# Unit tiles staggered by 64 bytes in on-chip memory, in a two-layer hybrid encoder

## The chip, the cores and the metric

The kernel runs on one core of one Trainium2 chip. The metric is the device time of one execution in microseconds (us), as the median of several runs. A profiled execution has a time of its own and a span, from its first to its last recorded instruction.

## The reference

The input x has 512 positions of 1024 float32 values. After a LayerNorm two layers follow, each with a mixing and a channel part:

```
h = layer_norm(x)
for l in 2 layers:
    proj = h @ w_in[l]                 # split into the inputs of four groups of 256 columns
    a = GLU -> depthwise conv of width 31 -> LayerNorm -> silu
    b = attention, 4 query and 2 key heads of 64, RMS norm, 2-D rotary
    c = gated unit: u * (sgu_w @ LN(v) + bias), in chunks of 128 positions
    d = attention with low-rank q and k/v, 4 heads of 96
    h = LN(alpha * h + concat(a, b, c, d) @ w_out[l])
    up = depthwise conv of width 3 (h @ ffn_w_up[l])       # 2 x 2816 columns
    h = LN(alpha * h + (silu(up[:, :2816]) * up[:, 2816:]) @ ffn_w_down[l])
```

## The kernel before, in words

**Products.** Every large product is made three times from numbers split in two: `split` (ACT copies a float32 tile into a rounded tile `hi`; DVE, or POOL for a few, subtracts to get the rest, `lo`), and `mm3` (three matmuls on TensorE: hi x hi, hi x lo, lo x hi, into one PSUM bank). The normalised stream stands transposed in `hh` and `hl` (128 partitions, 8 blocks of 512). In the feed-forward's first product (`ffn`, `col_mm`) a weight slice of 128 columns is the stationary operand (`wh`, `wl`) and a block of `hh` or `hl` the moving one, 512 columns long. In the second (`residual`, weights "W") the activations `fh` and `fl` are stationary and the weights move; part of these weights is kept in `hh` and `hl`, which are free by then (`load`). In attention, `att_pv` takes a 128-column slice of the value tile `bv` as the stationary operand; `b_attention` begins it at element 64*pr of the 192 elements that a key head has, so at bytes 0, 768, 256 and 1024 of the tile.

**Memory.** `Kern.__init__` opens pools in this order: const (with `h0` to `h3`), raws (3 slots of 4096 bytes per partition, where weights land from HBM), small, units, the two PSUM pools, and splits (`hh`, `hl`). The pool of units has 69 slots (`SLOTS["u"]`), nearly all other tiles live in it: split weights, activations, probabilities, row vectors. A tile never exceeds 2048 bytes per partition. In the compiled program of before, slot i begins at byte 53888 + 2048*i of each partition, so every unit begins 640 bytes past a multiple of 2048; `h0` to `h3` and the blocks of `hh` and `hl` begin at 640 too, the three raw slots at 1696.

**Order.** `Sched` records all operations, and `place` lays them out on five engines with costs, ranks and a window; it chooses the slot of each tile from a list of free slots that starts in the order of their numbers. `issue` then takes each tile from its pool under the tag of its slot (`u0` to `u68`, one buffer each) and issues the operations in the planned order, every one from the same line, L460. Planning takes no account of addresses.

Of the kernel before, what the change touches and what calls it, by code (L numbers as in the profile page):

```python
# [9 lines left out]
F32 = mybir.dt.float32  # L10
# [6 lines left out]
P = 128  # L17
# [39 lines left out]
SLOTS = {"u": 69, "raw": 3, "acc": 4, "wk": 4, "s": 48}  # L57
# [59 lines left out]
class View:  # L117


    def __init__(self, t, p0, p1, arr, chain):  # L120
        self.t, self.p0, self.p1, self.arr, self.chain = t, p0, p1, arr, chain
# [350 lines left out]
class Kern:  # L472
    def __init__(self, ctx, tc, x, wst, sguw, pp, rows, tabs, incol, out):
        nc = tc.nc
        self.x, self.wst, self.sguw, self.rows, self.out = x, wst, sguw, rows, out
        cp = ctx.enter_context(tc.tile_pool(name="const", bufs=1))
        PS = bass.MemoryType.PSUM
        pools = {"raw": ctx.enter_context(tc.tile_pool(name="raws", bufs=1)),
                 "s": ctx.enter_context(tc.tile_pool(name="small", bufs=1)),
                 "u": ctx.enter_context(tc.tile_pool(name="units", bufs=1)),  # L480
                 "acc": ctx.enter_context(tc.tile_pool(name="accs", bufs=1, space=PS)),
                 "wk": ctx.enter_context(tc.tile_pool(name="wks", bufs=1, space=PS))}

        sp = ctx.enter_context(tc.tile_pool(name="splits", bufs=1))
        self.s = Sched(tc, {k: (p, 0) for k, p in pools.items()})
        ident = cp.tile([P, P], F32, name="ident")
        make_identity(nc, ident)

        def fixed(shape, dt, name):
            return VTile(None, shape, dt, name, cp.tile(shape, dt, name=name))  # L490
        self.ident = VTile(None, [P, P], F32, "ident", ident)
        self.h = [fixed([P, DM], F32, f"h{t}") for t in range(NT)]
        self.hh, self.hl = [VTile(None, [P, KD, S], FR, n, sp.tile([P, KD, S], FR, name=n)) for n in ("hh", "hl")]
        self.pp, self.tabs = fixed([P, L * NPP], F32, "pp"), fixed([P, NT, 192], F32, "tabs")
        self.incol, self.incol_in = fixed([P, 2 * KD], F32, "incol"), incol
        self.pp_in, self.tabs_in = pp, tabs
        self.loaded = {}
# [846 lines left out]
```

## Time and profile before

| | |
|---|---|
| median of three runs | 1199.14 us (1197.52 to 1200.43) |
| profiled execution, its own time | 1199.15 us |
| its span | 1197.3 us |
| instructions | 15703, of which 5778 matmuls and 5778 weight loads |
| granted TensorE clock, mean | 0.991 |

PE is TensorE's matmuls, PEld its weight loads, DVE VectorE, ACT ScalarE, POOL GpSimd. The span counts from the first instruction recorded; the time of the execution is a little longer. In a timeline a matmul's duration covers its whole way through the array, so that the durations of neighbours overlap; what a matmul takes from the engine is the distance between starts.

### The profile page before, as it was taken

What the parts mean: (1) busy time and instruction counts of PE and PEld (TensorE: products, weight loads), DVE (VectorE), ACT (ScalarE), POOL (GpSimd) and SP (SyncE); (2) the same over time, 40 slices, a digit from 0 to 9 for tenths busy, and PEclk for the clock granted to TensorE, in tenths of its full rate; (3) what the DMA queues carried; (4) which work ended last, traced back from release to release, by engine and by line L of the source; (5) the groups of instructions that cost most, each with busy time, mean ns of one, the idle gap of its engine ahead of it and who ended that gap; (6) DMA issues with size and microseconds to landing.
All of it is one profiled execution on the core that took longest, in us unless ns stands there. A gap on an engine that the chain in (4) does not pass through costs nothing.

```text
span 1197.3 us, 15703 instructions
## 1 busy us (share of the span) xinstructions
PE 1147.8 (96%) x5778; PEld 962.6 (80%) x5778; DVE 830.4 (69%) x1546; ACT 558.1 (47%) x1193; POOL 216.0 (18%) x242
## 2 busy tenths in 40 slices
PE   5999998999999999999999999899999999999997
PEld 4787776898888888888898877779888888888886
DVE  8799899787666555525487999979766666661426
ACT  4657686335444443413224679752544444441221
POOL 5245666200000000000001467530000000000001
PEclk8999999999999999999999999999999999999999
DMA  8410211223422222333421201121333323331311
GB/s 301 134 54 1 88 54 54 89 71 123 141 88 97 81 71 75 122 103 108 139 80 62 71 1 53 37 88 54 124 105 98 96 90 105 100 97 50 106 53 71
DMA packets 32044, 105.74 MB, mean 88 GB/s; under 512 B 3680, under 2 KB 4064, under 8 KB 31968
## 3 DMA queue, kind: packets, MB, share of 16 engines
q1 hardware_dynamic: 31968, 104.74, 27.0%
q8 instruction: 45, 0.74, 0.3%
q14 instruction: 31, 0.25, 0.1%
HBM read 102.63 MB, written 2.10 MB: 87 GB/s over the span
## 4 chain that ended last, share of the span: by engine, by line
PE 77%; DVE 16%; ACT 4%; issue 2%; POOL 1%; DMA 0%; SPq 0%; DVEq 0%; ACTq 0%; POOLq 0%
PE acc L460 50%; PE wk L460 27%; DVE aconv L460 5%; DVE ptl L460 2%; DVE max L460 2%; DVE nu L460 1%; DVE wl L460 1%; DVE ny L460 1%; ACT by L460 1%; DVE h L460 1%; ACT prob L460 1%; POOL bw L460 1%; ACT pth L460 0%; DVE c L460 0%; DVE bst L460 0%
## 5 line engine op out<-in xcount | busy, mean ns | idle before, releaser
L460 DVE TENSOR_TENSOR wl<-raw,wh 128x512 fp32r<-128x512 f32 (+1 forms) x264 | 174.0, 690 | 64.9 <-ACT wh L460 50.2
L460 ACT ACTIVATE wh<-raw 128x512 fp32r<-128x512 f32 (+2 forms) x310 | 176.4, 615 | 43.6 <-DMA raw<-in_wst_dram 21.7
L460 PE MATMUL acc<-hl,wh 128*128 128x512 f32 (+1 forms) x544 | 191.6, 352 | 1.7 <-DVE hl L460 1.6
L460 PE MATMUL acc<-hh,wh 128*128 128x512 f32 (+1 forms) x544 | 191.8, 353 | 0.2 <-ACT hh L460 0.2
L460 PE MATMUL acc<-hh,wl 128*128 128x512 f32 (+1 forms) x544 | 191.3, 352 | 0.0
L460 POOL TENSOR_TENSOR wl<-raw,wh 128x512 fp32r<-128x512 f32 (+1 forms) x46 | 62.9, 1384 | 472.9 <-ACT wh L460 459.9
L460 PE MATMUL wk<-hh,wh 128*128 128x512 f32 x320 | 124.5, 389 | 0.0
L460 PE MATMUL wk<-hl,wh 128*128 128x512 f32 x320 | 124.5, 389 | 0.0
L460 PE MATMUL wk<-hh,wl 128*128 128x512 f32 x320 | 124.5, 389 | 0.0
L460 PEld LDWEIGHTS acc<-hl,wh 128*128 128x128 f32 x544 | 102.8, 189 | 16.4 <-DVE hl L460 2.6
L460 PEld LDWEIGHTS acc<-hh,wh 128*128 128x128 f32 x544 | 102.8, 189 | 14.3 <-ACT hh L460 0.5
L460 PEld LDWEIGHTS acc<-hh,wl 128*128 128x128 f32 x544 | 102.8, 189 | 13.7
L460 DVE SCALAR_TENSOR_TENSOR y<-acc,pp,y 128x511 f32<-128x511 f32 x96 | 71.9, 749 | 55.3 <-ACT y L460 54.0
L460 DVE TENSOR_TENSOR hl<-raw,hh 128x512 fp32r<-128x512 f32 x56 | 38.1, 691 | 93.2 <-ACT hh L460 93.2
L460 DVE SCALAR_TENSOR_TENSOR aconv<-aglu,pp,aconv 128x502 f32<-128x502 f32 (+14 forms) x120 | 94.6, 811 | 0.3
L460 DVE SCALAR_TENSOR_TENSOR y<-wk,pp,y 128x511 f32<-128x511 f32 x80 | 59.9, 749 | 46.2 <-ACT y L460 45.1
L460 PE MATMUL acc<-hl,fh 128*128 128x512 f32 x224 | 85.8, 383 | 0.0
L460 PE MATMUL acc<-hh,fh 128*128 128x512 f32 x224 | 85.7, 383 | 0.0
L460 PE MATMUL acc<-hh,fl 128*128 128x512 f32 x224 | 85.7, 382 | 0.0
L460 ACT ACTIVATE hh<-raw 128x512 fp32r<-128x512 f32 x56 | 34.8, 630 | 107.2 <-PE acc L460 66.1
L460 POOL TENSOR_TENSOR prob<-prob,rec 128x512 f32<-128x512 f32 x64 | 71.5, 1130 | 54.2 <-DVE rec L460 44.8
L460 POOL TENSOR_TENSOR h<-h,row 128x512 f32<-128x512 f32 x6 | 9.3, 1576 | 389.4 <-DVE h L460 389.4
(194 smaller groups left out, 2436.4 us busy)
## 6 DMA issues: line engine op xcount, KB each, us to landing
raw<-in_wst_dram SPq DMA_DIRECT2D x172, 512.0 KB, 3.5
row<-in_rows_dram SPq DMA_DIRECT2D x16, 256.0 KB, 6.4
raw<-in_wst_dram SPq DMA_DIRECT2D x8, 352.0 KB, 3.2
out_dram<-h SPq DMA_DIRECT2D x8, 256.0 KB, 2.0
h<-in_x_dram SPq DMA_DIRECT2D x3, 512.0 KB, 5.3
raw<-in_wst_dram SPq DMA_DIRECT2D x2, 384.0 KB, 3.9
h<-in_x_dram SPq DMA_DIRECT2D x2, 256.0 KB, 3.0
sgurow<-in_rows_dram SPq DMA_DIRECT2D x2, 256.0 KB, 5.8
```

The costliest lines, as they stand in the source:

```text
L460: f(*[a.real() if isinstance(a, View) else a for a in args], **{k: v.real() if isinstance(v, View) else v for k, v in kw.items()})
```

## The change

A loop behind the pools takes, ahead of all other tiles, one tile of 2048 bytes for each slot of the pool of units, under the slot's tag, and after slots 2, 5, 8, ... 59 a further tile of 64 bytes under a tag of its own. Neither is written or read. Slot i thus lies 64 bytes further for every such tile ahead of it: slots 0 to 2 as before, 3 to 5 by 64 bytes, and so on to slots 60 to 68 by 1280. The pool of splits, which follows, moves by 1280 bytes.

```diff
@@ -480,6 +480,11 @@
                  "u": ctx.enter_context(tc.tile_pool(name="units", bufs=1)),
                  "acc": ctx.enter_context(tc.tile_pool(name="accs", bufs=1, space=PS)),
                  "wk": ctx.enter_context(tc.tile_pool(name="wks", bufs=1, space=PS))}
+
+        for i in range(SLOTS["u"]):
+            pools["u"].tile([P, 512], F32, tag=f"u{i}", name=f"home{i}", bufs=1)
+            if i % 3 == 2 and i < 60:
+                pools["u"].tile([P, 16], F32, tag=f"gap{i}", name=f"gap{i}", bufs=1)
 
         sp = ctx.enter_context(tc.tile_pool(name="splits", bufs=1))
         self.s = Sched(tc, {k: (p, 0) for k, p in pools.items()})
```

## Rows read from the trace of the kernel before

**Rows 1.** The page: busy us and instructions by engine; the chain that ended last.

```profile
PE 1147.8 (96%) x5778; PEld 962.6 (80%) x5778; DVE 830.4 (69%) x1546; ACT 558.1 (47%) x1193; POOL 216.0 (18%) x242
...
PE 77%; DVE 16%; ACT 4%; issue 2%; POOL 1%; DMA 0%; SPq 0%; DVEq 0%; ACTq 0%; POOLq 0%
```

**Rows 2.** The table of stretches: a mixing stage and the two feed-forward stages.

```profile
core 0: us, PE busy (x) PEld busy (x) DVE busy (x) ACT busy (x) POOL busy (x), PEclk, DMA share, GB/s
100.00:200.00 100.00, 90.66 (x518) 74.61 (x518) 94.52 (x196) 73.53 (x171) 61.03 (x64) 0.97 0.17 53
250.00:600.00 350.00, 349.41 (x1626) 292.53 (x1625) 198.20 (x306) 135.44 (x222) 0.00 (x0) 1.00 0.32 104
850.00:1150.00 300.00, 300.00 (x1347) 249.29 (x1347) 168.39 (x249) 120.74 (x197) 0.00 (x0) 1.00 0.31 98
```

**Rows 3.** Timeline of PE, 400 to 410 us: the first and last of 44 starts.

```profile
start us, us, engine line op out<-in xcount [idle before <-releaser]
400.03 0.39 PE L460 MATMUL acc<-hh,wh 128*128 128x512 f32 x1
400.25 0.39 PE L460 MATMUL acc<-hl,wh 128*128 128x512 f32 x1
400.48 0.39 PE L460 MATMUL acc<-hh,wl 128*128 128x512 f32 x1
...
409.77 0.39 PE L460 MATMUL wk<-hl,wh 128*128 128x512 f32 x1
```

**Rows 4.** The table of stretches again: two short ones, at either level of the clock.

```profile
14.00:18.60 4.60, 4.60 (x13) 3.62 (x12) 4.04 (x8) 1.63 (x3) 4.60 (x5) 0.50 0.99 371
400.00:410.00 10.00, 10.00 (x45) 8.26 (x44) 5.28 (x8) 4.87 (x8) 0.00 (x0) 1.00 0.20 73
```

**Rows 5.** Timeline of PE, 14.2 to 19.9 us; six starts left out.

```profile
15.02 0.63 PE L460 MATMUL wk<-wh,hl 128*128 128x512 f32 x1
15.45 0.63 PE L460 MATMUL wk<-wh,hh 128*128 128x512 f32 x1
...
18.01 0.63 PE L460 MATMUL wk<-wh,hh 128*128 128x512 f32 x1
18.44 0.63 PE L460 MATMUL wk<-wl,hh 128*128 128x512 f32 x1
...
19.25 0.39 PE L460 MATMUL wk<-wh,hh 128*128 128x512 f32 x1
19.48 0.40 PE L460 MATMUL wk<-wl,hh 128*128 128x512 f32 x1
19.72 0.39 PE L460 MATMUL wk<-wh,hl 128*128 128x512 f32 x1
```

**Rows 6.** Instructions on tiles fh, fl, hh and hl: count, duration ns min/median/max.

```profile
L460 ACT ACTIVATE fh<-y x44: 615/633/634, 273.0 to 1073.5; 128x512 fp32r<-128x512 f32 x44
L460 DVE TENSOR_TENSOR fl<-y,fh x44: 678/692/694, 273.7 to 1074.2; 128x512 fp32r<-128x512 f32 x44
...
L460 ACT ACTIVATE hh<-raw x56: 615/632/634, 499.6 to 1144.2; 128x512 fp32r<-128x512 f32 x56
L460 DVE TENSOR_TENSOR hl<-raw,hh x56: 674/693/694, 500.3 to 1144.8; 128x512 fp32r<-128x512 f32 x56
```

**Rows 7.** Timeline of PE, attention times values, 702.3 to 704.1 us; four starts left out.

```profile
702.87 0.28 PE L460 MATMUL wk<-pth,bv 128*128 128x256 f32 x1
702.99 0.28 PE L460 MATMUL wk<-ptl,bv 128*128 128x256 f32 x1
703.11 0.28 PE L460 MATMUL wk<-pth,bv 128*128 128x256 f32 x1
703.23 0.28 PE L460 MATMUL wk<-ptl,bv 128*128 128x256 f32 x1
...
703.83 0.28 PE L460 MATMUL wk<-pth,bv 128*128 128x256 f32 x1
703.95 0.28 PE L460 MATMUL wk<-ptl,bv 128*128 128x256 f32 x1
```

## The prediction

> **What bounds the kernel now.** I read the page's busy shares and its chain first, then a table of stretches, then the TensorE timeline inside one stretch, because a change of addresses alone can act only through the length of single instructions. PE is busy for 96% of the span and the chain that ended last is 77% PE; DVE holds 16% of it [rows 1]. The table shows two stretches, 250 to 600 us and 850 to 1150 us, which are the two feed-forward stages: PE is busy for 649.4 of 650 us there, while DVE works 56% of the time, ACT 39% and POOL not at all [rows 2]. Nothing but the matmul rate sets the time of these 650 us. In the attention and convolution stages the same table has DVE at 94.5% and PE at 90.7% (100 to 200 us), so a gain of PE alone would be only partly paid there [rows 2].
>
> What one matmul costs is its pitch, the time from one start to the next; the duration in the timeline is longer because matmuls overlap. From 400.03 to 409.77 us there are 44 starts of 512-column matmuls, so 43 steps in 9.74 us: 226.5 ns each [rows 3]. In this stretch the granted clock was 1.00, the 2.4 GHz level [rows 4]; 512 columns at one per cycle are 213.3 ns. So each matmul carries about 13.3 ns more than its columns (226.67 ns is 544 cycles, and the starts are that regular). From 14.0 to 18.6 us the granted clock was 0.50, the 1.2 GHz level [rows 4], and eight steps from 15.02 to 18.44 us take 427.5 ns each, against 426.7 ns for 512 columns at that rate: within the rounding of the starts there is no surplus [rows 5]. The 13.3 ns therefore exists only when the moving operand streams at the full rate. That is the one place in this trace where operand addresses could be at work: a weight load (PEld, 80% busy beside PE's 96% [rows 1]) runs next to the matmuls, and both read the same partitions.
>
> **The change, part by part.** *The home tiles.* They fix slot i of the pool as the i-th 2048 bytes. The slots were already 2048 bytes apart and were first taken in the order of their numbers (the planner's free list starts sorted), so slot i keeps its place apart from the gaps. No instruction writes or reads a home or gap tile, so the real tile that follows one in a slot finds nothing to wait for; the planner never sees them, so order, slots, DMAs and semaphores stay. Cost 0, with nothing moved past any queue. If a tile did wait, it would be once per slot, at its first use, and there is no earlier work in the slot to wait on.
>
> *The gaps.* There are 20 of 64 bytes. Slot i shifts by 64 times the number of gaps ahead of it, and the last pool (hh, hl) by 1280. Before, every unit, hh, hl and every row block of h started 640 bytes past a multiple of 2048. Afterwards a unit's phase is 640 + 64g, with g from 0 to 20, and hh and hl have 1920.
>
> *DVE, ACT and POOL.* Their operands change phase against each other. The trace has both arrangements already. In fl<-y,fh all three operands have one phase; in hl<-raw,hh the source lies 1056 bytes off. DVE's medians are 692 and 693 ns; ACT's, for fh<-y and hh<-raw, 633 and 632 ns [rows 6]. A relative shift costs or gives under 1 ns in these pairs, so I enter 0. The bounds are plus and minus 1 ns on 1546 DVE instructions [rows 1], that is 1.5 us, were all of them on the path.
>
> *DMA.* Starts stay multiples of 64 bytes, the weight stream goes to the unshifted raw pool, and the DMA engines are 20% busy in the stretch of [rows 4] at 400 us. Cost 0; if a transfer took longer, a share of this size hides it.
>
> *TensorE against the other engines.* In the 10 us of [rows 3] DVE was busy for 5.28 and ACT for 4.87 us [rows 4], on units of the very same phase as the operands that PE reads, and the pitch did not move. I see no collision to remove here: 0.
>
> *TensorE against itself.* This is the open term. Afterwards the moving operand and the stationary one mostly have different phases. The nearest row is the attention's product with the values. There the stationary slice of the second head begins 768 bytes further into its tile than that of the first, with the moving tiles in the same phase. The first head's last step (702.87 to 702.99 us) and the second's seven from 703.11 to 703.95 us are all 120 ns [rows 7]. That is 106.7 ns for 256 columns at full rate and the same 13.3 ns; so a shift of 768 bytes leaves the surplus exactly, and so does halving the columns. Shifts of 64, 128 and 192 bytes have no row. The bounds: from minus 13.3 ns per matmul (the surplus goes) to plus 13.3 ns (it doubles). On the 5778 matmuls [rows 1] that is 77 us either way, an upper bound that also counts the transposes. I take the nearest row: 0.
>
> A page of the Trainium skill would set the floor elsewhere. TensorE: Matmul & The Clock Gate, section "Wait — 56ns, not 53.3ns?", gives N ÷ 2.4 GHz plus about 2.5 ns for back-to-back matmuls, 215.7 ns at 512 columns. The trace here disagrees, with 226.5 ns; its estimate for the half rate (426.7 ns) agrees. If the difference of 10.8 ns were all due to the phases and went in all 2973 matmuls of the two stretches, the kernel would be 32 us faster; that is rival A with this page's floor.
>
> **Sum:** 0 + 0 + 0 + 0 against the profiled execution's 1199.15 us (span 1197.3 and 1.85 us around it), which equals the median of the three runs, 1199.14, to 0.01 us. I forecast 1199.1 us.
>
> **The rivals.** *A, the surplus goes (faster).* Moving operand and weights collide in some unit of memory because their phases are equal, and different phases part them. For it: the surplus shows at the full rate alone, as a clash of two readers would. Against it: it is the same to the nanosecond for 256 and 512 columns and for the 768-byte shift, which looks like a fixed cost of changing weights. Price: since 768 bytes change nothing, a power of two at which phases repeat is at most 256; of the 69 slots 24 then still agree with hh and hl (g = 0, 4, 8, 12, 16 with three slots each, and the nine from slot 60 on), 45 differ, 65%. Of 2973 matmuls in the two PE-bound stretches [rows 2] that is 2973 x 0.65 x 13.3 ns = 25.7 us; over all 5778, 50 us. So 1149 to 1173 us, about 1165 with the other stages paying half. Were only one phase in three relieved, 9 us in the two stretches: 1190 us.
>
> *B, the shifted phases clash more (slower).* The weights of the next matmul are fetched while the moving operand streams; with equal phases the two may now keep out of each other's way for most of the time. Pitches above 227 ns do occur: 230 and 240 ns just after the clock rose, from 19.25 to 19.72 us [rows 5]. If half the surplus again, 6.7 ns, fell on the 65%, that is 2973 x 0.65 x 6.7 ns = 12.9 us in the two stretches: 1212 us. It decides once the pitch rises by 0.8 ns on average (2.4 us over 2973). Against it, again, the 768-byte row.
>
> *C, the change does not do what it says.* Should the allocator round or reorder slots so that the phases stay equal, the time is 1199 us as well; I give it 0.03, which lies inside the forecast's chance.
>
> **How the numbers follow.** A measurement of this kernel can tell about 0.2% (2.4 us) from no change; the three runs span 0.24%. No effect, C included, gets 0.72: the rows of DVE, ACT and the 768-byte shift all say that phases do not matter, but none of them has a 64-byte step. A gets 0.17, its full size 0.11 and its small one 0.06; B gets 0.11, of which about half would end under 1208 us. The likeliest case alone spans 1196.5 to 1201.8 us. To leave out no more than 2 in 10, the range takes in A's small form and B's smaller half: 1188 to 1208 us, which leaves out 0.11 and about 0.06.
>
> **What would show it.** Right: in 400 to 410 us of the new trace the step is again 226.5 ns with 44 or 45 starts; the loads, the medians of fl, hl, fh and the two fully busy stretches keep their lengths to 0.2%. A would show as steps between 213 and 220 ns for some weights and 226.5 for others, and B as steps of 230 ns or more, with PE still busy throughout. A new wait ahead of the first tile of a slot, or DVE medians off by more than 1 ns, would prove the other zeros wrong.

## The result, and the profile after

The changed kernel takes 1212.4 us (median of four runs, 1211.37 to 1214.8) against 1199.77 us before (median of four runs by then): a ratio of 1.0111 with a 95% interval of 1.0091 to 1.0132. (The ratio is estimated from the single runs; the two medians alone give 1.0105.) It is slower by 12.6 us, and the time lies above the range's upper end of 1208 us. I had forecast no change; what came is rival B, at its price of 1212 us.

The page of the changed kernel, busy us by engine and the shares of the chain that ended last:

```profile
PE 1161.5 (96%) x5778; PEld 961.3 (79%) x5778; DVE 830.1 (69%) x1546; ACT 558.3 (46%) x1193; POOL 215.8 (18%) x242
...
PE 80%; DVE 14%; ACT 3%; issue 2%; POOL 1%; DMA 0%; SPq 0%; DVEq 0%; ACTq 0%; POOLq 0%
```

Against [rows 1], PE has changed: 13.7 us more, with the same 5778 matmuls. The weight loads have 1.3 us less; DVE, ACT and POOL agree to 0.3 us, and PE's share of the chain has gone from 77 to 80%. The span grew by 13.3 us, from 1197.3 to 1210.6. The table of stretches shows it as a lower rate:

```profile
core 0: us, PE busy (x) PEld busy (x) DVE busy (x) ACT busy (x) POOL busy (x), PEclk, DMA share, GB/s
...
250.00:600.00 350.00, 349.41 (x1595) 287.64 (x1594) 193.00 (x291) 135.32 (x222) 0.00 (x0) 1.00 0.32 104
850.00:1150.00 300.00, 300.00 (x1336) 245.31 (x1335) 167.84 (x247) 119.33 (x194) 0.00 (x0) 1.00 0.29 93
```

PE waits no more than before [rows 2] and the granted clock is 1.00 in both, but fewer matmuls fit. The timeline of PE from 400 to 410 us, first and last of the starts and a few between:

```profile
400.19 0.40 PE L460 MATMUL acc<-hl,wh 128*128 128x512 f32 x1
400.42 0.40 PE L460 MATMUL acc<-hh,wl 128*128 128x512 f32 x1
400.67 0.40 PE L460 MATMUL acc<-hh,wh 128*128 128x512 f32 x1
...
402.75 0.39 PE L460 MATMUL acc<-hh,wh 128*128 128x512 f32 x1
402.97 0.39 PE L460 MATMUL acc<-hl,wh 128*128 128x512 f32 x1
...
409.91 0.40 PE L460 MATMUL wk<-hl,wh 128*128 128x512 f32 x1
```

The 42 steps from 400.19 to 409.91 us average 231.4 ns where [rows 3] have 226.5, and they are no longer equal: 250 ns in one place and 220 in another, in the rows shown. I took the same instructions out of both traces, by their place in PE's order: the 2743 matmuls of 512 columns that lie in the two stretches of the kernel before have a mean pitch of 226.8 ns there and of 231.2 ns now. That is 4.5 ns each and 12.3 us together, of the 13.3 us by which the span grew. Sorted by the distance between the weights that are being loaded and the operand that is moving (addresses from the compiled program, modulo 256), the means away from the stages' borders are 230.1 ns at 0, 232.8 at 64, 232.4 at 128 and 230.5 at 192; before, all were at 0 with 226.7. Where the border is drawn moves these means by about 0.2 ns. The matmuls at distance 0 are of two kinds: in 260 to 590 and 860 to 1140 us, the 415 that come straight after another distance average 232.6 ns, and the 223 with seven or more at distance 0 in front of them 226.7.

The zeros entered for the other engines stand. Instructions on hh, hl, fh and fl, duration min/median/max:

```profile
L460 ACT ACTIVATE fh<-y x44: 614/632/634, 271.9 to 1084.8; 128x512 fp32r<-128x512 f32 x44
L460 DVE TENSOR_TENSOR fl<-y,fh x44: 681/692/695, 272.5 to 1085.4; 128x512 fp32r<-128x512 f32 x44
...
L460 ACT ACTIVATE hh<-raw x56: 612/632/635, 502.6 to 1156.9; 128x512 fp32r<-128x512 f32 x56
L460 DVE TENSOR_TENSOR hl<-raw,hh x56: 674/692/694, 503.3 to 1157.6; 128x512 fp32r<-128x512 f32 x56
```

The medians of [rows 6] are met to 1 ns.

### The profile page after: what moved, and what is told of

Same layout as the page of the kernel before. It is cut to its first block, busy times and chain, and to the rows that moved or that the text cites. A ratio compares the mean times of both kernels' runs of the same rounds, so it can differ in the third digit from the quotient of the medians.

```text
span 1210.6 us, 15703 instructions
## 1 busy us (share of the span) xinstructions
PE 1161.5 (96%) x5778; PEld 961.3 (79%) x5778; DVE 830.1 (69%) x1546; ACT 558.3 (46%) x1193; POOL 215.8 (18%) x242
## 4 chain that ended last, share of the span: by engine, by line
PE 80%; DVE 14%; ACT 3%; issue 2%; POOL 1%; DMA 0%; SPq 0%; DVEq 0%; ACTq 0%; POOLq 0%
PE acc L460 51%; PE wk L460 29%; DVE aconv L460 3%; DVE ptl L460 2%; DVE max L460 2%; DVE nu L460 1%; DVE ny L460 1%; ACT by L460 1%; DVE h L460 1%; DVE wl L460 1%; POOL bw L460 1%; DVE mixl L460 0%; ACT prob L460 0%; DMA raw<-in_wst_dram 0%; DVE c L460 0%
```

## The experiments

Three theories went in. **Phase:** a matmul's cost depends on the distance, modulo 256 bytes, between the stationary slices and the moving slices. **Mixture:** only a change of that distance from one matmul to the next costs. **Other engines:** VectorE's or ScalarE's accesses disturb TensorE in the new layout.

The encoder runs were made in two sets, each beside runs of its own of the kernel before: 25 with a median of 1199.76 us, 7 with 1200.75.

**One distance at a time, nothing else running.** A kernel of chains of 96 matmuls of 512 columns, rounded float32 as in the encoder, each chain with its own PSUM name:

```
for c, (name, a, b) in enumerate(CONF):
    ...
    nc.tensor.matmul(ps, w[:, ws + j * 128:ws + j * 128 + 128], m[:, ms + k * 512:ms + k * 512 + 512], ...)
```

> The encoder's work is left out; only chains of 96 matmuls of 512 columns run, each chain with one distance in bytes between the stationary slice and the moving slice that is read beside it. Phase theory (what a matmul costs depends on that distance modulo 256): chains at distance 0 and 256 have a pitch of 226.7 ns, those at 64, 128 and 192 of about 231 to 234 ns, as the new trace has them. Mixture theory (only a change of the distance from one matmul to the next costs): all chains of one distance have 226.7 ns, the three that alternate between two distances 230 to 234 ns. Other-engines theory (VectorE's or ScalarE's accesses disturb TensorE): all chains 226.7 ns, since no other engine works.

The lines view, grouped by name, with count, then busy us and mean ns of one:

```profile
L39 PE MATMUL wj<-mov,stat 128*128 128x512 f32 x96 | 22.6, 395 | 0.0
...
L39 PE MATMUL wg<-mov,stat 128*128 128x512 f32 x96 | 22.6, 395 | 0.0
L39 PE MATMUL xg<-mov,stat 128*128 128x512 f32 x96 | 22.5, 394 | 0.0
...
L39 PE MATMUL mj<-mov,stat 128*128 128x512 f32 x96 | 22.5, 394 | 0.0
...
L39 PE MATMUL xl<-mov,stat 128*128 128x512 f32 x96 | 22.2, 392 | 0.0
L39 PE MATMUL mg<-mov,stat 128*128 128x512 f32 x96 | 22.2, 391 | 0.0
L39 PE MATMUL wl<-mov,stat 128*128 128x512 f32 x96 | 22.1, 391 | 0.0
L39 PE MATMUL wa<-mov,stat 128*128 128x512 f32 x96 | 21.9, 389 | 0.0
L39 PE MATMUL wn<-mov,stat 128*128 128x512 f32 x96 | 21.9, 389 | 0.0
L39 PE MATMUL wo<-mov,stat 128*128 128x512 f32 x96 | 21.9, 389 | 0.0
```

The stationary slice is shifted by 0 (wa), 64 (wg), 128 (wj), 192 (wl), 240 (wn) and 256 bytes (wo); in mg and mj the moving slice is shifted by 64 and 128 instead, and xg and xl alternate between 0 and 64 and between 0 and 192. A chain's busy time is 95 steps and one duration, so wa has (21.9 - 0.39) / 95 = 226.4 ns and wg 233.7. The granted clock was 1.00 in 60 to 65 and in 170 to 175 us. From the starts themselves, after the first 30: 226.66 at 0, 240 and 256, 233.29 at 64, 233.40 at 128, 228.85 at 192, and 228.92 for mg. The vector, scalar and GpSimd engines do no work in these chains, so they are not needed for the cost; a constant distance costs, which mixture denied; and mg agrees with wl, as a distance of -64 should with 192. One pair does not agree as well: with the moving slice shifted by 128 the pitch is 232.34 ns, with the stationary one 233.40, so the distance modulo 256 is not quite all that counts. Mixing costs as well. The chain that alternates 0 and 64 has 232.46, less than the constant 64 but 2.5 ns above the mean of the two constant chains, and the one that alternates 0 and 192 has 229.94, more than either of its parts. Phase and mixture are thus both at work. The two stretches of the changed kernel have 39, 22, 19 and 19% of their long matmuls at 0, 64, 128 and 192; with the sweep's pitches for these the mean would be 229.9 ns. By this estimate the distances alone give 3.2 of the 4.5 ns, and their mixture the other 1.3.

**hh and hl alone moved.**

```diff
         sp = ctx.enter_context(tc.tile_pool(name="splits", bufs=1))
+        sp.tile([P, 16], F32, name="gap")
```

> The kernel before, with hh and hl alone moved by 64 bytes; all units keep one phase. Phase theory: every matmul with hh or hl as the moving or the stationary operand beside a unit has a distance of 64 or 192 bytes, pitch in the first feed-forward product about 233 ns, 20 to 26 us slower than before (1220 to 1226 us). Mixture theory: distance constant, pitch 226.7 ns, time of before within 2.4 us. Other-engines theory: units untouched against each other, time of before within 2.4 us.

Measured: 1203.34 us against 1199.76, ratio 1.0031 (1.0018 to 1.0044), so slower by 3.6 us (2.2 to 5.3 by the interval), where mixture and other engines had no change, but far under the 20 to 26 us that I had written. I had reckoned with the pitch at 64; the weights now lie 64 bytes behind, at distance 192, where the sweep has 228.85 ns. The encoder's pitch there is 228.9 ns, over 2022 matmuls at that distance away from the stages' borders. The expectation had the wrong sign of the shift; with the right one the size follows. The 512-column matmuls of the two stretches take 5.6 us more in all, and the 256-column ones pay some of it back: those that follow one another, about 840 in the kernel, have a mean pitch of 117.7 ns instead of 119.7.

**The units alone moved,** the same step in the other direction (hh and hl keep their phase by a shift of 256 in all):

```diff
+        pools["u"].tile([P, 16], F32, tag="gap", name="gap", bufs=1)
         sp = ctx.enter_context(tc.tile_pool(name="splits", bufs=1))
+        sp.tile([P, 48], F32, name="gap")
```

> The units alone moved by 64 bytes against hh and hl (which stay in their phase modulo 256): the distance of weights to moving operand in the first feed-forward product is 64 bytes where the run with hh and hl moved had 192. Phase theory with the first sweep's pitch of 233.3 ns at 64: about 16 to 20 us slower than before, 1216 to 1220 us. Mixture theory: one distance throughout, so at most the 4 us of the run with hh and hl moved. Other-engines theory: as before.

Measured: 1214.47 against 1200.75 us, ratio 1.0109 (1.0089 to 1.0129). The sign of a 64-byte step thus makes 3.6 or 13.7 us. Its pitch at distance 64 is 233.34 ns over 2033 matmuls, as in the sweep to 0.05 ns; the total is 2 us under what I had expected, which priced 256-column matmuls like the long ones, and those came out faster (121.6 ns instead of 125.2 over the 162 of the first stretch).

**Everything moved alike.**

```diff
+        pools["u"].tile([P, 16], F32, tag="gap", name="gap", bufs=1)
         sp = ctx.enter_context(tc.tile_pool(name="splits", bufs=1))
```

> The kernel before, with the units and hh, hl all moved by the same 64 bytes: relative distances of TensorE's operands as before, absolute addresses changed, and also the distance to the raw slots and to the h tiles. Phase and mixture theory: pitch 226.7 ns, time of before within 2.4 us. A theory in which the absolute address counts, or the distance to the raw slots: 8 to 13 us slower, as the changed kernel.

Measured: 1200.51 against 1199.76 us, ratio 1.0004 (0.9993 to 1.0015), pitch 226.67 ns. For a shift by 64 bytes, the absolute address and the distance to raw and h tiles do not count.

**Five gaps of 256 bytes, and five of 64.** Two kernels, the change with other gaps:

```diff
-            if i % 3 == 2 and i < 60:
-                pools["u"].tile([P, 16], F32, tag=f"gap{i}", name=f"gap{i}", bufs=1)
+            if i % 12 == 11 and i < 60:
+                pools["u"].tile([P, 64], F32, tag=f"gap{i}", name=f"gap{i}", bufs=1)
```

> The change with five gaps of 256 bytes (after slots 11, 23, 35, 47, 59) in place of twenty of 64: the same 1280 bytes in all, the units in six phases modulo 2048 but in one phase modulo 256. Phase and mixture theory with a period of 256 bytes: pitch 226.7 ns, time of before within 2.4 us. If the period is 512 bytes or more: pitch above 227 ns on the part of the slots that differ, 5 to 13 us slower.

The second has `[P, 16]` in the last line.

> The partner of the run with five gaps of 256 bytes: the same five places, 64 bytes each. Phase theory with a period of 256: the units have distances 192, 0, 64, 128, 192, 0 to hh and hl, in blocks of twelve slots, so a pitch of 230 to 232 ns and 9 to 13 us more than before (1209 to 1213 us). A theory in which the number or place of the gaps counts and not their size: as the run with 256 bytes, 1200 us.

With 256 bytes 1199.97 against 1199.76 us, ratio 1.0002 (0.999 to 1.0013); with 64 bytes 1212.39 against 1200.75, ratio 1.0096 (1.0075 to 1.0117), both as the phase theory had them. The table of stretches from 300 to 400 us, where PE does nothing but 512-column matmuls, gives the whole family: first 256-byte gaps, then 64-byte gaps, then the units alone moved, then hh and hl alone, one fence each.

```profile
300.00:400.00 100.00, 100.00 (x442) 82.78 (x442) 63.14 (x92) 44.95 (x74) 0.00 (x0) 1.00 0.35 111
```

```profile
300.00:400.00 100.00, 100.00 (x435) 81.37 (x434) 62.18 (x92) 44.17 (x72) 0.00 (x0) 1.00 0.33 106
```

```profile
300.00:400.00 100.00, 100.00 (x430) 80.60 (x429) 61.14 (x90) 44.10 (x72) 0.00 (x0) 1.00 0.33 106
```

```profile
300.00:400.00 100.00, 100.00 (x439) 82.05 (x438) 62.16 (x91) 44.94 (x74) 0.00 (x0) 1.00 0.35 109
```

The numbers of matmuls are 442, 435, 430 and 439. The kernel before has 443 in this stretch and the changed kernel 434, as these rows of the same view show, before first:

```profile
300.00:400.00 100.00, 100.00 (x443) 82.80 (x442) 63.44 (x92) 44.63 (x74) 0.00 (x0) 1.00 0.34 109
```

```profile
300.00:400.00 100.00, 100.00 (x434) 81.26 (x433) 61.95 (x91) 44.18 (x72) 0.00 (x0) 1.00 0.33 106
```

The size of a gap decides, not its being there, and steps of 256 bytes count as none.

**All distances in steps of 4 bytes.** The sweep again with 64 chains, and four of 256 columns:

> The encoder's work is left out; chains of 72 matmuls, one for each shift of the stationary slice by 0, 4, 8, ... 252 bytes (names qaa, qab, ... qdp, four letters a to d for each 64 bytes and sixteen a to p for each 4), and four chains of 256 columns (na to nd, shifts 0, 64, 128, 192). Phase theory: 226.7 ns at 0 and at 240, 228.9 at 192, 232 to 234 at 64, 128 and 160 as in the first sweep, and the chains of 256 columns show the same surplus in ns over 106.7 ns. If the cost is a clash that some distance avoids altogether, one chain lies well under 226.7 ns, down to 213 to 216 ns; if equal phases are the best case there is, none lies under 226 ns.

The lines view, names as in the expectation (qaa is 0 bytes, qae 16, qbo 120, qcj 164; na to nd 0, 64, 128, 192 bytes with 256 columns):

```profile
L35 PE MATMUL qcj<-mov,stat 128*128 128x512 f32 x72 | 17.2, 400 | 0.0
...
L35 PE MATMUL qae<-mov,stat 128*128 128x512 f32 x72 | 17.0, 395 | 0.0
...
L35 PE MATMUL qbo<-mov,stat 128*128 128x512 f32 x72 | 16.5, 389 | 0.0
...
L35 PE MATMUL qaa<-mov,stat 128*128 128x512 f32 x72 | 16.5, 389 | 0.0
...
L35 PE MATMUL na<-mov,stat 128*128 128x256 f32 x72 | 8.8, 283 | 0.0
L35 PE MATMUL nc<-mov,stat 128*128 128x256 f32 x72 | 8.7, 281 | 0.0
L35 PE MATMUL nd<-mov,stat 128*128 128x256 f32 x72 | 8.6, 279 | 0.0
L35 PE MATMUL nb<-mov,stat 128*128 128x256 f32 x72 | 8.3, 276 | 0.0
```

After the first 20 starts of each chain, none of the 64 distances has a mean pitch under 226.66 ns. Eight share that floor (0, 120, 132, 144, 156, 204, 228 and 252 bytes), the worst is 237.16 at 164, and 30 lie between 233.2 and 233.5. Shift and surplus follow no simple curve: 128 and 136 bytes have 233.4 and 233.3 ns, 132 the floor. Nor is the pitch a function of the distance alone: at 240 bytes it is 228.3 ns here and was 226.66 in the first sweep, each throughout a chain. For 256 columns the order turns over, where the expectation had the same surplus at each distance as for 512: 119.94 ns at 0, 113.33 at 64, 118.69 and 117.78 at 128 and 192. So the old layout is at the best case found for long matmuls, and rival A had nothing to win on them.

**Narrower weights.** Chains at distance 0 and 64 with 128, 96, 64 and 32 stationary columns; against the kernel of the 64 chains the matmul is:

```diff
-                nc.tensor.matmul(ps[:, 0:n], w[:, ws + j * 128:ws + j * 128 + 128], m[:, k * 512:k * 512 + n],
+                nc.tensor.matmul(ps[0:n, :], w[:, ws + j * 128:ws + j * 128 + n], m[:, k * 512:k * 512 + 512],
```

> The encoder's work is left out; chains of 96 matmuls of 512 columns whose stationary slice has 128, 96, 64 or 32 columns (512, 384, 256, 128 bytes per partition), each at distance 0 and 64 (sa and sb 128 columns, sc and sd 96, se and sf 64, sg and sh 32, si again 128 at distance 0). Read-clash theory (the weight load's reads take turns with the moving operand's, so each read of weights can cost one stall): the 13.3 ns above 213.3 ns shrink in proportion, 10, 6.7 and 3.3 ns at distance 0 (or down to the smallest surplus that a change of weights has), and the 6.7 ns more at distance 64 shrink with them. Fixed-cost theory (a change of weights costs 13.3 ns whatever is read): 226.7 ns for every width at distance 0.

Measured at distance 0: 226.68, 230.02, 230.05 and 231.71 ns; at 64: 233.38, 228.34, 232.66 and 231.71. Neither theory holds. The weight load itself gets shorter, as the lines view shows for 128 and 32 columns (count, busy us, mean ns):

```profile
L35 PEld LDWEIGHTS sa<-mov,stat 128*128 128x128 f32 x96 | 18.0, 188 | 3.7
...
L35 PEld LDWEIGHTS sg<-mov,stat 128*32 128x32 f32 x96 | 10.5, 109 | 11.8
```

but at distance 0 the surplus does not shrink with it; it grows from 13.3 to 18.4 ns. At 64 it goes up and down: 20.0, 15.0, 19.3 and 18.4 ns. What the surplus is made of therefore stays open. That it depends on the distance of the two operands is shown; that reads of weights take turns with reads of the moving operand, each costing a step, is not, and in the simple form tried here it is refuted.

## Why the prediction was wrong, point by point

**What bounds the kernel** was right: the two stretches are paid in full by the matmul rate, and 12.3 of the 13.3 us fell there. The surplus of 13.3 ns at the full clock was the right place to look, and the sign named for B, steps of 230 ns or more with PE busy throughout, is what most of 400 to 410 us showed.

**Home tiles, DVE, ACT, POOL and DMA at zero** were right: the same instruction counts, medians within 1 ns, 1200 us for gaps of 256 bytes, which bring the same home tiles and 57 shifted slots where the change has 66. So was the zero for TensorE against the other engines: the units moved alone gave the encoder, with DVE and ACT at work, the pitch of the bare chain to 0.05 ns.

**"TensorE against itself", taken at 0, is the step that failed.** I took the nearest row, the attention's 768-byte shift [rows 7]. But 768 is three times 256, and under both rivals, as I priced them myself, phases repeat at 256 bytes: the row is one more case of equal phases and says nothing about 64, 128 and 192. Its agreement weighed as evidence for no effect in the chances, where it could not tell the cases apart. In place of the 0 the runs showed a cost that depends on the distance of the two operands: 226.66 ns at 0, 233.3 at 64, 233.4 at 128 and 228.9 at 192 in chains of one distance, and in the changed kernel, where distances follow one another, a price for the matmuls at distance 0 too. That came to plus 4.5 ns on the long matmuls and 12.3 us in the two stretches. It lies inside the bounds of plus and minus 13.3 ns; a value between them, with a wider range, was all that the rows allowed.

**Rival B** named the mechanism's place and nearly its parts: half the surplus, 6.7 ns, at a shifted phase. The sweep has 6.6 ns at 64 and 6.7 at 128, though 2.2 at 192. The 65% was wrong in kind: matmuls at distance 0 cost 3.5 ns more too (230.1 ns) in the changed kernel, while in a kernel or chain that keeps distance 0 throughout they cost no more. Neighbours at other distances make that, as the alternating chains show, and as the 232.6 against 226.7 ns inside the changed kernel do. The price of 6.7 ns was too high for the shifted matmuls, and the 35% entered at nothing was too low; that the two errors cancel, so that 12.9 us were priced for the two stretches and 12.3 came, is luck in the sum. B's chance of 0.11 rested on the 768-byte row and was too low for a case that no row spoke against. The reason that I gave for B (with equal phases the two keep out of each other's way) is in keeping with the sweep, where distance 0 is at the floor, and is not shown beyond that.

**Rival A** read the same surplus as something that a layout could take away. 64 distances say no for 512 columns; for 256 columns 6.6 of the 13.3 ns do go, at 64 bytes. The floor of N ÷ 2.4 GHz plus about 2.5 ns that the Trainium skill gives (TensorE: Matmul & The Clock Gate, "Wait — 56ns, not 53.3ns?"), 215.7 ns at 512 columns, was not met by any chain of 512 columns here: 226.66 ns was the least, 11.0 ns over it.

**No faster version followed.** The long matmuls are, before the change, at the least pitch that any chain showed. To put only the 256-column ones at 64 bytes would need slots of their own; it wasn't tried.

## What to carry to other kernels

Where a trace holds only one arrangement of addresses, a regular pitch says nothing about other arrangements; and a shifted case is evidence only if its shift is no multiple of the period that one suspects. A chain of a hundred matmuls per distance, with nothing else in the kernel, gave in one run the pitch of an encoder that keeps one distance, to 0.1 ns; it does not give that of a layout in which distances mix. For back-to-back rounded-float32 matmuls of 512 columns, start stationary and moving tiles at the same offset modulo 256 bytes, or keep padding to multiples of 256: the same gaps cost nothing in that size and 1% at 64 bytes.

## What the runs showed of the hardware that was not expected

The pitch of one constant stream depends on the byte distance of its operands, from 226.66 to 237.16 ns at 512 columns, and often settles in short cycles: at 128 bytes steps of 229 and 237 ns take turns, at 64 steps of 231 and 236. All steady means lie between a floor of 544 cycles of the 2.4 GHz level and some 570, 560 (233.33 ns) being the commonest; four bytes of shift can decide between 544 and 560, and at 240 bytes two chains settled differently, at 226.66 and 228.3 ns. They ran in two kernels on two chips, after other chains; which of this decides is not shown. Matmuls of 256 columns have another best distance (64 bytes, 113.33 ns) than those of 512 (0). Narrower weights did not make a 512-column matmul cheaper at distance 0; at 64 bytes 96 stationary columns took 228.34 ns where 128 took 233.38. Moving both operands alike by 64 bytes changed nothing, and the busy times of DVE, ACT and POOL stayed within 0.3 us in the new layout. Why the distance of the two operands costs TensorE time is open.
